# The first input of a two-layer kernel in eight stages of two column tiles, with keys and half of the values between the modulation units

## The chip, the cores and the metric

The kernel runs on one core of a Trainium2 chip. The metric is the time of the device for one execution, in microseconds (us). All matrix work is in fp32, done as three products of a reduced fp32 format, so one multiplication of a tile is three instructions on TensorE (PE). ScalarE (ACT) and VectorE (DVE) prepare operands and collect sums; the queue of SyncE (SP) issues nearly all loads from the chip's memory.

## The reference

Two layers run over a sequence of 256 rows (`x`) beside a context of 256 rows (`ctx`), both 2048 wide. Each layer first makes a shift, a scale and a gate out of a small condition vector, by a product with `w_ada` (2048 x 6144 per layer). Layer 0 is a gated linear attention with a short convolution; of the context it needs only the end states.

```python
m = jax.nn.silu(cond) @ w[:, :n * D_MODEL] + b[:n * D_MODEL]       # modulation
u  = x * (1.0 + sc) + sh            ;  uc = ctx_s * (1.0 + sc_c) + sh_c
k, v, rf, rb, q, ... = split_cols(u @ w_in_e[0], E_SIZES)          # keys 1024, values 1024, ranks 32, ...
s_f, s_b = context_states(uc @ w_in_e[0][:, :E_STATE_COLS], ...)   # keys, values, ranks of ctx
y  = even_mixer(u @ w_in_e[0], s_f, s_b, ...)   ; x = layer_norm(alpha * x + gt * y, ...)
y  = odd_mixer(u1 @ w_in_o[0], w_pool, ...)     ; x = layer_norm(alpha * x + gt * y, ...)
```

## The kernel before

The change lies in the first phase, which makes keys, ranks and a part of the values of layer 0, for `x` and `ctx` together. It walks over the 2048 input columns in tiles of 128 (16 tiles, `kt`). A **stage** is one or two of these tiles. `STAGES` gives their widths: one, one, and then seven times two.

For one stage, `stage_u` does the following. `mod_rows` (L274) multiplies the condition vectors with the stage's columns of `w_ada`, in **units** of 1 MB; a stage of two tiles has four units of eight tiles of 256 columns each, a stage of one tile has two units of sixteen tiles of 128 columns. `to_cols` copies the sum to `arow` (L285, ACT), turns it with PE (`adaT`, L288), and two DVE instructions add the bias (`modT`, L293 and L295). PE transposes the `x` and `ctx` columns (`px`, L389 and L390). ACT and DVE then make u (L392, L393), and split it into a high and a low part (`uxh`, `uch` on ACT L397 and L398; `uxl`, `ucl` on DVE L399 and L400). After every four tiles PE makes the four rank products (`pr`, L405), each in two passes.

`stage_k` makes the keys: for two halves of 512 columns and four blocks of rows, three instructions per tile (`kacc`, L190 to L192), so 24 per tile and 48 per stage of two. The weights come as raw loads and are split by ACT (`wh`, L152) and DVE (`wl`, L153). The sums are copied by ACT in the first stage (`knat`, L423), and added by DVE in the others (L425).

A **fill** (`v_fill`) multiplies two tiles with the first 512 columns of the values, 24 instructions (`vfill`), with its own split weights (`swh`, `swl`) and its sums in `vnat` (L454 copies on ACT, L456 adds on DVE). There are four fills, for the first eight tiles; the other eight tiles of these columns are done behind the first phase (`vacc`). Behind the first phase follow the turned keys (`nT`, L684), values, queries, gates, the recurrence, the output products and layer 1. The modulation of layer 1 and the gate of layer 0 are a background of 1 MB loads, each with four DVE sums (`aacc`, L533).

The raw loads of `w_ada` and of all weights (L138) go in one order through the queue of SP into a pool of four raw buffers of 1 MB; a load waits until its buffer's last reader is done. A scheduler lays the instructions of each engine into one order before the run, by priorities and by explicit "issue after" edges; on the chip each engine keeps that order.

## Time and profile before

| what | value |
|---|---|
| median of 3 runs | 1011.63 us (1009.72 to 1018.11) |
| the profiled execution | 1005.89 us, its span 1004.1 us |
| granted TensorE clock, mean of the span | 0.995 |
| TensorE busy | 958.9 us, 95% |
| VectorE busy | 807.0 us, 80% |
| ScalarE busy | 468.9 us, 47% |
| moved by DMA | 255.44 MB, mean 254 GB/s |

Times in the trace count from the start of the span. The times "start to start" of two matmuls matter more here than their durations, because matmuls overlap. A wait of an engine is the idle time ahead of an instruction, put down to what released it.

### The profile page before, as it was taken

To read this page: it belongs to the slowest core of one execution; us is meant where nothing else is said; L and a number is where in the kernel's file an instruction comes from. 1 tells how busy PE (TensorE), PEld (TensorE's weight loads), DVE (VectorE), ACT (ScalarE), POOL (GpSimd) and SP (SyncE) were. 2 spreads that over 40 slices of the span, in tenths; PEclk is the share of its full clock that TensorE was granted. 3 is DMA by queue.
4 is the path that set the end of the run, shared out by engine and by line. 5 is a ranking of instruction groups with operands and counts; after the bars stand their busy time and mean duration, and the time that the engine had idled before them with its cause. 6 is when DMAs were issued, how large, how long until landed. Compare 5 with 4: busy or idle time off the path is not lost.

```text
span 1004.1 us, 14346 instructions
## 1 busy us (share of the span) xinstructions
PE 958.9 (95%) x5654; PEld 757.0 (75%) x5654; DVE 807.0 (80%) x1172; ACT 468.9 (47%) x643; POOL 24.4 (2%) x56
## 2 busy tenths in 40 slices
PE   5899999999999999999999999999989999989995
PEld 4566756778878877877888788888778777768885
DVE  1555646989996999799999879997979997666676
ACT  2422214356675676246463344345745555435340
POOL 2000000000000000000000000000010001000000
PEclk9999999999999999999999999999999999999998
DMA  9987899567787586757766897985598998875532
GB/s 264 328 263 257 289 290 339 188 242 235 260 300 262 179 268 218 257 195 258 248 215 226 299 309 263 327 303 200 175 354 288 309 333 317 264 282 190 178 117 84
DMA packets 150371, 255.44 MB, mean 254 GB/s; under 512 B 5078, under 2 KB 46720, under 8 KB 150304
## 3 DMA queue, kind: packets, MB, share of 16 engines
q1 hardware_dynamic: 146592, 245.13, 72.5%
q0 software_dynamic: 2896, 8.72, 2.9%
q8 instruction: 44, 0.72, 0.3%
q10 hardware_dynamic: 816, 0.68, 0.3%
q14 instruction: 23, 0.19, 0.0%
HBM read 252.41 MB, written 2.10 MB: 253 GB/s over the span
## 4 chain that ended last, share of the span: by engine, by line
PE 49%; DVE 29%; DMA 15%; issue 4%; ACT 2%; SPq 0%; DVEq 0%; ACTq 0%
DMA raw<-in_w_ada_dram 12%; DVE wl L153 10%; DVE aacc L533 7%; PE oacc L190 5%; PE oacc L191 5%; PE oacc L192 5%; PE xacc L192 5%; PE xacc L191 5%; PE xacc L190 5%; PE ada L274 2%; DMA raw<-in_w_in_o_dram 2%; PE kacc L190 2%; PE kacc L192 2%; PE kacc L191 2%; PE pr L405 1%
## 5 line engine op out<-in xcount | busy, mean ns | idle before, releaser
L152 ACT CAST wh<-raw 128x1024 fp32r<-128x1024 f32 (+1 forms) x250 | 257.2, 1044 | 249.4 <-PE xacc L192 74.5
L153 DVE TENSOR_TENSOR wl<-raw,wh 128x1024 fp32r<-128x1024 f32 (+1 forms) x250 | 298.0, 1210 | 46.7 <-ACT wh L152 44.2
L533 DVE SCALAR_TENSOR_TENSOR aacc<-raw,sil,aacc 128x512 f32<-128x512 f32 x240 | 179.3, 747 | 30.8 <-DMA raw<-in_w_ada_dram 27.1
L190 PE MATMUL xacc<-wh,uxh 128*128 128x512 f32 x384 | 152.6, 397 | 0.0
L192 PE MATMUL xacc<-wh,uxl 128*128 128x512 f32 x384 | 151.5, 395 | 0.0
L191 PE MATMUL xacc<-wl,uxh 128*128 128x512 f32 x384 | 150.2, 391 | 0.5 <-DVE wl L153 0.4
L191 PEld LDWEIGHTS xacc<-wl,uxh 128*128 128x128 f32 x384 | 72.2, 188 | 16.3 <-DVE wl L153 1.3
L190 PEld LDWEIGHTS xacc<-wh,uxh 128*128 128x128 f32 x384 | 72.1, 188 | 15.5 <-ACT wh L152 0.5
L192 PEld LDWEIGHTS xacc<-wh,uxl 128*128 128x128 f32 x384 | 72.1, 188 | 15.3 <-issue 0.2
L425 DVE TENSOR_TENSOR knat<-kacc,knat 128x512 f32<-128x512 f32 x64 | 42.8, 685 | 34.7 <-PE kacc L192 34.5
L285 ACT COPY arow<-ada 128x256 f32<-128x256 f32 (+1 forms) x9 | 3.1, 349 | 100.6 <-PE ada L274 100.6
L274 PE MATMUL ada<-raw,sil 128*32 128x256 f32 (+1 forms) x576 | 36.2, 382 | 10.8 <-DMA raw<-in_w_ada_dram 10.8
L190 PE MATMUL xacc<-wh,u1h 128*128 128x512 f32 x112 | 44.9, 401 | 0.8 <-ACT u1h L1160 0.8
L190 PE MATMUL oacc<-wh,y1h 128*128 128x512 f32 (+1 forms) x120 | 45.5, 379 | 0.0
L191 PE MATMUL xacc<-wl,u1h 128*128 128x512 f32 x112 | 44.7, 399 | 0.5 <-DVE wl L153 0.4
L192 PE MATMUL oacc<-wh,y1l 128*128 128x512 f32 (+1 forms) x120 | 45.0, 375 | 0.0
L191 PE MATMUL oacc<-wl,y1h 128*128 128x512 f32 (+1 forms) x120 | 45.0, 375 | 0.0
L192 PE MATMUL xacc<-wh,u1l 128*128 128x512 f32 x112 | 44.5, 397 | 0.0
L274 PEld LDWEIGHTS ada<-raw,sil 128*32 128x32 f32 x576 | 17.4, 118 | 27.0 <-issue 12.0
L190 PE MATMUL kacc<-wh,uxh 128*128 128x512 f32 x64 | 26.8, 418 | 1.5 <-ACT uxh L397 1.5
L1221 PE MATMUL xacc<-wh,dm 128*128 128x512 f32 x64 | 25.7, 402 | 2.5 <-ACT wh L152 2.5
L190 PE MATMUL kacc<-wh,uch 128*128 128x512 f32 x64 | 26.4, 412 | 0.5 <-DVE knat L425 0.5
(339 smaller groups left out, 1866.6 us busy)
## 6 DMA issues: line engine op xcount, KB each, us to landing
raw<-in_w_ada_dram SPq DMA_DIRECT2D x96, 1024.0 KB, 6.3
raw<-in_w_in_e_dram SPq DMA_DIRECT2D x54, 1024.0 KB, 5.5
raw<-in_w_in_o_dram SPq DMA_DIRECT2D x32, 1024.0 KB, 7.2
raw<-in_w_out_e_dram SPq DMA_DIRECT2D x16, 1024.0 KB, 7.0
raw<-in_w_out_o_dram SPq DMA_DIRECT2D x16, 1024.0 KB, 5.1
raw<-in_w_in_e_dram SPq DMA_DIRECT2D x18, 512.0 KB, 7.0
raw<-in_w_pool_dram SPq DMA_DIRECT2D x4, 1024.0 KB, 7.7
gt<-in_b_ada_dram POOLq DMA_DIRECT2D x8, 256.0 KB, 4.1
```

The source lines that it names most:

```text
L152: nc.scalar.copy(h, r[:, j : j + w, :])
L153: nc.vector.tensor_tensor(out=l, in0=r[:, j : j + w, :], in1=h.bitcast(F32), op=ALU.subtract)
L190: nc.tensor.matmul(out=acc, lhsT=uh, rhs=wh, start=start, stop=False)
L191: nc.tensor.matmul(out=acc, lhsT=uh, rhs=wl, start=False, stop=False)
L192: nc.tensor.matmul(out=acc, lhsT=ul, rhs=wh, start=False, stop=stop)
L274: nc.tensor.matmul(out=ps[32 * g : 32 * g + 32, :], lhsT=sil[:, kt, 2 - 2 * half : 34 - 2 * half], rhs=r[:, j, :], start=half == 0 and kt ...
L285: arow_ins.append(nc.scalar.copy(a[:, :nw], ps))
L405: nc.tensor.matmul(out=pr[32 * g : 32 * g + 32, :], lhsT=wr[:, kk, :], rhs=quad_u[kk // 2][:, kk % 2, :], start=True, stop=True,)
L425: nc.vector.tensor_tensor(out=dst, in0=acc, in1=dst, op=ALU.add)
L533: e.scalar_tensor_tensor(out=a, in0=r[j], scalar=sc, in1=a, op0=ALU.mult, op1=ALU.add)
L1221: nc.tensor.matmul(out=accs[0], lhsT=dh, rhs=wh, start=f, stop=False)
```

## The change

The 16 tiles go in eight stages of two. There are eight fills, one for each stage, so the first 512 columns of the values are complete at the end of the first phase, and the two blocks of them behind it are gone. `stage_u` of the next stage is laid between the key and fill groups of the present one: `behind(unit)` puts each of its modulation units after a group that is given by `PLACE` (after 3/16, 6/16, 9/16 and 12/16 of the groups). The transposes come after the last unit but one of stage 0 and after the last unit in the others (with no explicit place for `adaT`), the rank products as one piece after the first group of the second key half. The loads of a stage's keys are issued ahead of its third unit's load (ahead of the fourth in stage 0). The splits of weights follow after the high parts of u. In the head, 25 products of a zero tile are put between the modulation units (`keep_warm`). One background unit (1 MB, four `aacc`) follows each of the stages 4 to 7.

```diff
-ADA_0 = {}
+ADA_0 = {i: 1 for i in range(4, 8)}
-FILLS = {2: [(0, 0, 2)], 4: [(0, 2, 2)], 6: [(0, 4, 2)], 8: [(0, 6, 2)]}
+FILLS = {k + 2: [(0, k, 2)] for k in range(0, KT, 2)}
+PLACE = 3
+STAGE_PRIO = 2000
-STAGES = (1, 1, 2, 2, 2, 2, 2, 2, 2)
+WARM = (7, 5, 3)
+STAGES = (2, 2, 2, 2, 2, 2, 2, 2)
...
+    def keep_warm(n, behind=None):
+        idle = mp([P, 256], "idle")
+        for _ in range(n):
+            with tc.issue_after(behind.ins) if behind else nullcontext():
+                nc.tensor.matmul(out=idle, lhsT=zero[:, 0:P], rhs=zero, start=True, stop=True)
...
-    def mod_rows(k0, n):
+    def mod_rows(k0, n, behind, between):
...
+                unit = half * (KT // nk) + kk // nk
+                if unit == 3 and k0 == 0:
+                    w_load(1)
+                elif unit == 2 and k0:
+                    w_load(min(len(specs), wst["u"] + 2))
                 r = load_unit(w_ada[0], kk, nk, c0, nw)
+                with behind(unit):
+                    for j in range(nk):
+                        kt = kk + j
+                        g = kt % 4
+                        ins = nc.tensor.matmul(
+                            out=ps[32 * g : 32 * g + 32, :], lhsT=sil[:, kt, 2 - 2 * half : 34 - 2 * half], rhs=r[:, j, :],
+                            start=half == 0 and kt < 4, stop=half == 1 and kt >= KT - 4,
+                        )
+                between(half, kk + nk, ins)
...
-    def stage_u(k0, n):
+    def stage_u(k0, n, groups):
...
+        pxs = {}
+
+        def transposes(j):
+            pxs[j] = mp([P, 512], "px")
+            for t in range(2):
+                nc.tensor.transpose(out=pxs[j][:, t * P : (t + 1) * P], in_=xs[:, t, j * P : (j + 1) * P], identity=ident)
+                nc.tensor.transpose(out=pxs[j][:, 256 + t * P : 256 + (t + 1) * P], in_=cs[:, t, j * P : (j + 1) * P], identity=ident)
+
+        def between(half, k, ins):
+            if (half, k) == (1, KT // 2 if k0 == 0 else KT):
+                with tc.issue_after(ins.ins):
+                    for j in range(n):
+                        transposes(j)
+            if k0 == 0:
+                keep_warm(WARM[2] if (half, k) == (1, KT) else WARM[1], ins)
+
+        def behind(unit):
+            if not groups:
+                return nullcontext()
+            return tc.issue_after(groups[(unit + 1) * len(groups) * PLACE // 16 - 1].ins)
+
...
         pt = to_cols(ps, w)
+        with tc.issue_after(arow_ins[-1].ins):
+            w_ahead(1, 1)
...
             if i == 3:
+                ranks_due.append(kt)
...
+        with tc.issue_after(behind.ins), prio(-2 * STAGE_PRIO):
+            first = product(3)
+            with tc.issue_after(first.ins):
+                for g in range(3):
+                    product(g)
...
+    def stage_k(k0, n, groups):
         for nb in range(2):
             parts = w_next((W_E, k0, n, nb * 512), 0, 0)
             for m in range(4):
                 acc = acc_bank("kacc")
                 for j in range(n):
-                    mm3(acc, utile(m, k0 + j), parts[j], j == 0, j == n - 1)
+                    ins = mm3(acc, utile(m, k0 + j), parts[j], j == 0, j == n - 1)
+                groups.append(ins)
+                if ranks_due and (nb, m) == (1, 0):
+                    ranks(ranks_due.pop(), ins)
...
+    starts = [sum(STAGES[:i]) for i in range(len(STAGES))]
+    groups = []
+    for i, (k0, n) in enumerate(zip(starts, STAGES)):
+        if i == 0:
+            stage_u(k0, n, [])
+            with tc.issue_after(h_ins[-1].ins):
+                w_ahead(3, 2)
+        if i + 1 < len(STAGES):
+            xcs[k0 + n] = load_xc(k0 + n, STAGES[i + 1])
+        groups = []
+        stage_k(k0, n, groups)
+        for f in FILLS.get(k0 + n, ()):
+            v_fill(*f, groups)
+        pump_ada(ADA_0.get(i, 0))
+        if i + 1 < len(STAGES):
+            with prio(-STAGE_PRIO):
+                stage_u(k0 + n, STAGES[i + 1], groups)
+                with tc.issue_after(h_ins[-1].ins):
+                    w_ahead(3, 2)
```

Three places show what this does to the order of the instructions; the names are tile and buffer numbers of the program.

In the queue of SP, at the start of the program, these loads stood before (the columns of `x` and `ctx` of the first stage go through another queue):

```order
L138 DMA raw_141<-in_w_ada_dram 128x16x128
L138 DMA raw_159<-in_w_ada_dram 128x16x128
L138 DMA raw_198<-in_w_in_e_dram 128x512
L138 DMA raw_204<-in_w_in_e_dram 128x512
L138 DMA raw_214<-in_w_ada_dram 128x16x128
L138 DMA raw_232<-in_w_ada_dram 128x16x128
L211 DMA xc_210<-in_x_dram 128x2x128
L212 DMA xc_210<-in_ctx_dram 128x2x128
```

and these stand there now:

```order
L141 DMA raw_151<-in_w_ada_dram 128x8x256
L141 DMA raw_167<-in_w_ada_dram 128x8x256
L141 DMA raw_183<-in_w_ada_dram 128x8x256
L141 DMA raw_209<-in_w_in_e_dram 128x2x512
L141 DMA raw_211<-in_w_ada_dram 128x8x256
L141 DMA raw_252<-in_w_in_e_dram 128x2x512
L141 DMA raw_258<-in_w_in_e_dram 128x2x512
L141 DMA raw_368<-in_w_ada_dram 128x8x256
L141 DMA raw_378<-in_w_ada_dram 128x8x256
```

All four units of stage 0 (`raw_151`, `raw_167`, `raw_183`, `raw_211`) come ahead of the first keys, where two units of half the columns came before; one key load of 0.5 MB (`raw_209`) lies among them. On DVE, the same place read before:

```order
L248 COPY colT<-pc_1_177 128x32
L293 SCALAR_TENSOR_TENSOR modT<-adaT_182,colT 128x2
L295 TENSOR_TENSOR modT<-adaT_182,colT 128x2
L153 TENSOR_TENSOR wl_201<-raw_198,wh_200 128x512
L153 TENSOR_TENSOR wl_207<-raw_204,wh_206 128x512
L393 TENSOR_SCALAR u_186<-px_187,modT 128x256
L399 TENSOR_TENSOR uxl_117<-u_186,uxh_116 128x256
L400 TENSOR_TENSOR ucl_119<-u_186,uch_118 128x256
```

and reads now:

```order
L156 TENSOR_TENSOR wl_234<-raw_209,wh_233 128x1024
L262 COPY colT<-pc_1_225 128x32
L314 SCALAR_TENSOR_TENSOR modT<-adaT_230,colT 128x2x2
L316 TENSOR_TENSOR modT<-adaT_230,colT 128x2x2
L435 TENSOR_SCALAR u_239<-px_193,modT 128x256
L435 TENSOR_SCALAR u_239<-px_198,modT 128x256
L441 TENSOR_TENSOR uxl_127<-u_239,uxh_126 128x256
L442 TENSOR_TENSOR ucl_129<-u_239,uch_128 128x256
```

The split `wl` of the first weights, 128x1024 in one, stands ahead of `colT` and `modT`, and there are two u instead of one ahead of the first low part. On ACT, in the order of the rows, the end of the first fill read before:

```order
L397 CAST uxh_116<-u_370 128x256
L152 CAST wh_489<-raw_487 128x1024
L398 CAST uch_118<-u_370 128x256
L454 COPY vnat_445<-vfill_449 128x512
L454 COPY vnat_446<-vfill_457 128x512
L454 COPY vnat_447<-vfill_465 128x512
L454 COPY vnat_448<-vfill_473 128x512
L285 COPY arow_542<-ada_496 128x256
L392 ACTIVATE u_549<-px_550,modT 128x256
L392 ACTIVATE u_549<-px_561,modT 128x256
L397 CAST uxh_120<-u_549 128x256
L398 CAST uch_122<-u_549 128x256
```

and reads now (`u_433` is the u of the stage 1, whose first keys come right behind `vfill_359` on PE):

```order
L511 COPY vnat_331<-vfill_335 128x512
L306 COPY arow_422<-ada_367 128x256
L155 CAST wh_427<-raw_388 128x1024
L511 COPY vnat_332<-vfill_343 128x512
L511 COPY vnat_333<-vfill_351 128x512
L511 COPY vnat_334<-vfill_359 128x512
L434 ACTIVATE u_433<-px_412,modT 128x256
L434 ACTIVATE u_433<-px_417,modT 128x256
L439 CAST uxh_126<-u_433 128x256
L440 CAST uch_128<-u_433 128x256
```

Three copies of the fill now stand between the split of the weights of stage 1 and its u. Before, the u of the keys that follow the fill (`u_370`) stood ahead of all four copies.

On DVE, at the stage whose modulation comes with the gate weights (`gate_weights`, `wp`), the rows before read:

```order
L293 SCALAR_TENSOR_TENSOR modT<-adaT_1286,colT 128x2x2
L295 TENSOR_TENSOR modT<-adaT_1286,colT 128x2x2
L425 TENSOR_TENSOR knat_134<-kacc_1330,knat_134 128x512
L425 TENSOR_TENSOR knat_135<-kacc_1338,knat_135 128x512
L153 TENSOR_TENSOR wl_1381<-raw_1378,wh_1380 128x1024
L425 TENSOR_TENSOR knat_132<-kacc_1346,knat_132 128x512
L425 TENSOR_TENSOR knat_133<-kacc_1354,knat_133 128x512
L425 TENSOR_TENSOR knat_134<-kacc_1362,knat_134 128x512
L153 TENSOR_TENSOR wl_1387<-raw_1384,wh_1386 128x1024
L425 TENSOR_TENSOR knat_135<-kacc_1370,knat_135 128x512
L437 TENSOR_TENSOR wp_1281<-wg_1276,wp_1281 32x1024
L393 TENSOR_SCALAR u_1291<-px_1292,modT 128x256
```

and now, with the fill of the stage before it (`vfill_1305` to `vfill_1329`) ahead:

```order
L513 TENSOR_TENSOR vnat_331<-vfill_1305,vnat_331 128x512
L488 MEMSET wg_1406 96x1024
L493 TENSOR_TENSOR wp_1403<-wg_1398,wp_1403 32x1024
L513 TENSOR_TENSOR vnat_332<-vfill_1313,vnat_332 128x512
L513 TENSOR_TENSOR vnat_333<-vfill_1321,vnat_333 128x512
L513 TENSOR_TENSOR vnat_334<-vfill_1329,vnat_334 128x512
L314 SCALAR_TENSOR_TENSOR modT<-adaT_1416,colT 128x2x2
L316 TENSOR_TENSOR modT<-adaT_1416,colT 128x2x2
L156 TENSOR_TENSOR wl_1420<-raw_1364,wh_1419 128x1024
L493 TENSOR_TENSOR wp_1411<-wg_1406,wp_1411 32x1024
L435 TENSOR_SCALAR u_1425<-px_1388,modT 128x256
```

Three adds of the fill stand ahead of `modT` now; the adds of keys that stood between `modT` and u are gone from there, and the split of the next keys' weights and the second `wp` stand in their place.

## Rows read from the trace of the kernel before

**Rows 1.** page, 1: busy time, share of the span and instructions of an engine

```profile
PE 958.9 (95%) x5654; PEld 757.0 (75%) x5654; DVE 807.0 (80%) x1172; ACT 468.9 (47%) x643; POOL 24.4 (2%) x56
```

**Rows 2.** page, 4: the chain of waits by engine

```profile
PE 49%; DVE 29%; DMA 15%; issue 4%; ACT 2%; SPq 0%; DVEq 0%; ACTq 0%
```

**Rows 3.** stretches: start:end, length, busy PE, PEld, DVE, ACT, POOL, PEclk, DMA, GB/s

```profile
16.95:194.24 177.29, 172.00 (x1117) 114.42 (x1118) 104.77 (x190) 49.95 (x91) 0.41 (x2) 1.00 0.88 284
64.00:86.00 22.00, 21.73 (x141) 14.52 (x141) 12.62 (x23) 5.46 (x10) 0.00 (x0) 1.00 0.87 286
```

**Rows 4.** waits of PE, ahead of 194.24 and behind: total us, times, longest

```profile
PE ada L274 <- DMA raw<-in_w_ada_dram: 10.8, 6, 4.6
...
PE yT L968 <- DVE y L962: 4.1, 3, 2.0
PE y1T L1279 <- DVE gate L1326: 3.3, 1, 3.3
```

**Rows 5.** the head in order of time: start us, us, instruction, idle before

```profile
11.99 1.30 PE L274 MATMUL ada<-raw,sil 128*32 128x128 f32 x20 [2.46 <-DMA raw<-in_w_ada_dram]
...
14.00 0.27 ACT L285 COPY arow<-ada 128x128 f32<-128x128 f32 x1 [9.54 <-PE ada L274]
...
14.16 1.14 ACT L152 CAST wh<-raw 128x512 fp32r<-128x512 f32 x2
15.09 1.28 DVE L153 TENSOR_TENSOR wl<-raw,wh 128x512 fp32r<-128x512 f32 x2
15.90 0.56 ACT L392 ACTIVATE u<-px,modT 128x256 f32<-128x256 f32 x1 [0.60 <-PE px L390]
16.49 0.40 ACT L397 CAST uxh<-u 128x256 fp32r<-128x256 f32 x1
16.95 0.80 PE L190 MATMUL kacc<-wh,uxh 128*128 128x512 f32 x1 [1.09 <-ACT uxh L397]
```

**Rows 6.** bytes moved from 0 to 45 us, in 40 slices of 1.125 us

```profile
GB/s 0 15 191 308 323 287 288 290 282 305 362 315 300 180 156 289 291 291 289 307 361 361 350 348 346 348 346 348 349 350 349 350 367 356 352 401 279 256 376 308
```

**Rows 7.** PE in two stages: start us, us, instruction

```profile
63.58 0.51 PE L288 MATMUL adaT<-sel,arow 128*128 128x4 f32 x4
64.77 0.48 PE L192 MATMUL kacc<-wh,uxl 128*128 128x512 f32 x1
65.78 0.39 PE L190 MATMUL kacc<-wh,uch 128*128 128x512 f32 x1
...
68.28 0.39 PE L192 MATMUL kacc<-wh,ucl 128*128 128x512 f32 x1
...
76.86 1.07 PE L274 MATMUL ada<-raw,sil 128*32 128x256 f32 x16
77.86 0.50 PE L192 MATMUL kacc<-wh,uxl 128*128 128x512 f32 x1
...
133.70 1.05 PE L405 MATMUL pr<-u,wr_acc 128*32 128x512 f32 x4
134.69 0.50 PE L190 MATMUL kacc<-wh,uch 128*128 128x512 f32 x1
```

**Rows 8.** the end of the first phase, PE

```profile
194.24 1.47 PE L684 MATMUL nT<-ident,knat 128*128 128x128 f32 x12
```

**Rows 9.** groups of the first phase: count, busy us, mean ns, idle before

```profile
L454 ACT COPY vnat<-vfill 128x512 f32<-128x512 f32 x4 | 2.3, 584 | 2.4 <-PE vfill L192 2.4
L456 DVE TENSOR_TENSOR vnat<-vfill,vnat 128x512 f32<-128x512 f32 x12 | 8.3, 689 | 2.5 <-PE vfill L192 2.4
L153 DVE TENSOR_TENSOR swl<-raw,swh 128x1024 fp32r<-128x1024 f32 x4 | 4.9, 1218 | 0.4 <-ACT swh L152 0.4
```

**Rows 10.** PE behind its longest wait of the later phases

```profile
884.35 1.09 PE L1279 MATMUL y1T<-ident,gate 128*128 128x128 f32 x8 [3.31 <-DVE gate L1326]
...
885.93 0.63 PE L192 MATMUL xacc<-wh,u1l 128*128 128x512 f32 x1
...
888.49 0.60 PE L192 MATMUL xacc<-wh,u1l 128*128 128x512 f32 x1
```

More of the change, by code (lines that the diff above doesn't have):

```diff
@@ L1 @@
 import math
-from contextlib import ExitStack, contextmanager
+from contextlib import ExitStack, contextmanager, nullcontext
 import concourse.bass as bass
@@ L191, in mm3 @@
         nc.tensor.matmul(out=acc, lhsT=uh, rhs=wl, start=False, stop=False)
-        nc.tensor.matmul(out=acc, lhsT=ul, rhs=wh, start=False, stop=stop)
+        return nc.tensor.matmul(out=acc, lhsT=ul, rhs=wh, start=False, stop=stop)
     rows0 = slot([32, P], F32, "rows0")
@@ L269, in mod_rows @@
             for kk in range(0, KT, nk):
-                r = load_unit(w_ada[0], kk, nk, c0, nw)
-                for j in range(nk):
-                    kt = kk + j
-                    g = kt % 4
-                    nc.tensor.matmul(
-                        out=ps[32 * g : 32 * g + 32, :], lhsT=sil[:, kt, 2 - 2 * half : 34 - 2 * half], rhs=r[:, j, :],
-                        start=half == 0 and kt < 4, stop=half == 1 and kt >= KT - 4,
-                    )
+                unit = half * (KT // nk) + kk // nk
[3 more added lines that the diff above has]
+                    w_load(min(len(specs), wst["u"] + 2))
+                r = load_unit(w_ada[0], kk, nk, c0, nw)
+                with behind(unit):
[7 more added lines that the diff above has]
+                between(half, kk + nk, ins)
         return ps
-    arow_ins = []
+    arow_ins, h_ins = [], []
     def to_cols(ps, nw):
@@ L370, in stage_u @@
         xs, cs = xc[:, 0:2, :], xc[:, 2:4, :]
-        ps = mod_rows(k0, n)
+        pxs = {}
[15 more added lines that the diff above has]
+            return tc.issue_after(groups[(unit + 1) * len(groups) * PLACE // 16 - 1].ins)
+        ps = mod_rows(k0, n, behind, between)
         if k0 == 0:
@@ L386, in stage_u @@
             u = quad_u[-1]
-            px = mp([P, 512], "px")
-            for t in range(2):
-                nc.tensor.transpose(out=px[:, t * P : (t + 1) * P], in_=xs[:, t, j * P : (j + 1) * P], identity=ident)
-                nc.tensor.transpose(out=px[:, 256 + t * P : 256 + (t + 1) * P], in_=cs[:, t, j * P : (j + 1) * P], identity=ident)
+            px = pxs[j]
             ux, uc = u[:, kt % 2, 0:256], u[:, kt % 2, 256:512]
@@ L401, in stage_u, with ranks, product @@
             if i == 3:
-                pr = mp([P, 512], "pr")
-                for g in range(4):
-                    kk = kt - 3 + g
-                    nc.tensor.matmul(
-                        out=pr[32 * g : 32 * g + 32, :], lhsT=wr[:, kk, :], rhs=quad_u[kk // 2][:, kk % 2, :],
-                        start=True, stop=True,
-                    )
-                if q == 0:
-                    nc.vector.tensor_copy(r_acc, pr)
-                else:
-                    nc.vector.tensor_tensor(out=r_acc, in0=pr, in1=r_acc, op=ALU.add)
-    def stage_k(k0, n):
+                ranks_due.append(kt)
+    ranks_due = []
+    def ranks(kt, behind):
+        pr = mp([P, 512], "pr")
+        def product(g):
+            kk = kt - 3 + g
+            return nc.tensor.matmul(
+                out=pr[32 * g : 32 * g + 32, :], lhsT=wr[:, kk, :], rhs=quad_u[kk // 2][:, kk % 2, :], start=True, stop=True)
+        with tc.issue_after(behind.ins), prio(-2 * STAGE_PRIO):
[3 more added lines that the diff above has]
+                    product(g)
+        if kt == 3:
+            nc.vector.tensor_copy(r_acc, pr)
+        else:
+            nc.vector.tensor_tensor(out=r_acc, in0=pr, in1=r_acc, op=ALU.add)
+    def stage_k(k0, n, groups):
         for nb in range(2):
@@ L440, with v_fill @@
     vnat = []
-    def v_fill(nb, kt, nk):
+    def v_fill(nb, kt, nk, groups):
         parts = w_next((W_E, kt, nk, 1024 + nb * 512), 0, 0)
@@ L450, in v_fill @@
                 for j in range(nk):
-                    mm3(acc, utile(m, kt + j), parts[j], j == 0, j == nk - 1)
+                    ins = mm3(acc, utile(m, kt + j), parts[j], j == 0, j == nk - 1)
+                groups.append(ins)
                 dst = vnat[m][:, nb * 512 : (nb + 1) * 512]
@@ L771 @@
     for nb in range(2):
+        if not V_Q[nb]:
+            continue
         accs = [acc_bank("vacc") for _ in range(4)]
```

21 lines of the change are left out of this document (4 added, 17 removed).

## Prediction

> **What bounds the kernel.** I read the page first: TensorE is busy for 95% of the span [rows 1], and it is the largest share of the chain of waits, with DVE at 29% and DMA at 15% [rows 2]. Next I looked at the first phase by stretches, since the edit is there: from the first key product at 16.95 to the first turned key at 194.24 [rows 8] PE is busy for 172.0 of 177.3 us, at full granted clock [rows 3]. The waits of PE say where the rest is: modulation units that wait for their load, 10.8 us in six waits [rows 4]. 4.6 us of that is the longest, ahead of the first unit, and 2.5 us the next, ahead of the second [rows 4, 5]; so only some 3.7 us of load waits lie inside the phase. The timeline gives prices: twelve instructions of keys start between 65.78 and 68.28, one each 0.227 us [rows 7]. That is the price of a matmul here, not its duration of 0.39.
>
> So PE is packed, and a change of order can win only the head, the slow clock at its end, and the small waits. Let me count what these are. Behind 16.95 the phase holds 384 key products (87.2 us), 96 of fills (21.8), 30 units of modulation at 1.1 (33.0), seven blocks and two half blocks of transposes (about 10.4), and four rank groups at 3.3 (13.2): 165.6 us. 177.3 - 165.6 = 11.7 us is lost, and 16.95 us ahead of it.
>
> **Prices, step by step.**
>
> *Point of comparison.* The change moves 96 value products from behind the phase into it, at 0.227 each 21.8 us. Later they are missing, so they cost nothing in sum, as long as PE is packed in both places. The equal of 194.24 is then 216.0.
>
> *Head.* Four units of 1.05 MB now come ahead of the first key product, with 0.52 MB of keys, 0.52 MB of `x` and `ctx` and, by their shapes, 0.37 MB of rank weights and small rows: 5.6 MB. The slices of bytes moved add up to 3.34 MB at 13.5 us [rows 6]. The other 2.26 MB take 6.5 us at the 349 GB/s of the later slices, 7.5 at 300: 20.0 to 21.0. If the whole head went at 349 from 3.4 us on, it would be 18.8. I take 20.2, and 1.0 for the unit on PE [rows 7]: 21.2. From there, the chain. In the trace of before it took 2.95 us from `arow` to the first key product [rows 5]. Now DVE's split of 1.22 us (the `swl` of the same size) [rows 9] stands ahead of `modT` and itself waits for ACT's split of about 1.05 (two halves took 1.14) [rows 5]. Summed: `arow` 0.4, 1.05, 1.22, column copy and `modT` 0.5, u 0.56 and the second one 0.5, `uxh` 0.46 until the product starts: 4.7. First key product at 25.9, with bounds of 24.5 and 27.5.
>
> *Work behind it.* Keys 87.2; fills, now 192 products, 43.6; 28 units at 1.00 from start to next start and 0.1 at the switch into them, 30.8 [rows 7]; seven blocks of `adaT` and transposes at 1.19 and 0.1, 9.1 [rows 7]. The rank products came in three pieces of 1.0 to 1.1 per group (the first piece 0.99) [rows 7]; as one piece I put 2.5, between 2.0 and 3.3: 10.0. Sum 180.7.
>
> *New waits.* Each engine keeps its order. At the end of the first fill ACT has three copies of the fill ahead of u of stage 1, whose keys follow at once: last copy 0.58 [rows 9], u 0.56 and 0.5, `uxh` 0.4 [rows 5], hand-overs: 2.2 us. At the gate weights, DVE's add of the last fill block, 0.69 [rows 9], is ahead of `modT`, and then the same chain: 2.8 us. Before, keys that needed none of this covered both. Three smaller ones are read alike: 1.3 between stages 4 and 5, where the background's sums stand ahead; 1.3 ahead of the last fill, for its split of 1.22 [rows 9]; 1.7 for loads in stage 6, about one wait of the kind that was 10.8 / 6 = 1.8 [rows 4]. The other borders I put at 0.7 together. Sum 10.0. The bounds are 4 (only the two chains, half covered by products already queued) and 18 (each of the six other borders as long as the shorter chain, less overlap).
>
> *The 25 zero products.* They fill waits for loads of the head, where PE had 4.6 and 2.5 us of idle time [rows 4, 5]: nothing. If they delayed each unit by one of them, it would be under 1 us, inside the bounds of the head. What they are to bring is the clock. Behind a wait of 3.31 us PE's products started 0.427 us apart (885.93 to 888.49, six starts) instead of 0.227 [rows 10, 7], for eight instructions in a row: 1.6 us. The wait at the end of the head is of that kind (4.7 us with about 1.5 us of transposes, zero products and `adaT` inside); I put half of 1.6, so 0.8, with ends of 0 and 1.6. [...]
>
> *Moved DVE and ACT work.* 16 more adds of the fills, eight fewer of the keys and four fewer of the values, at 0.69: +2.8 us of DVE, and four background units are summed earlier; DVE is busy for 12.6 of 22.0 us in such a stage [rows 3], so this is covered, and so are ACT's 5.5 of 22.0.
>
> *Later phases.* They lose 96 products and what stands with them. Waits for DVE there are short (4.1 and 3.3 us in the two largest groups) [rows 4]. I take 0, with ends of -4 and +3.
>
> *Sum.* 25.9 + 180.7 + 10.0 = 216.6, against 216.0: +0.6; with the clock +1.4. The profiled execution took 1005.9 us, so 1007.3; the median of the runs shown stands 5.7 us above that execution, so as a median **1013.0 us**. The differences that this kernel's measurement can tell from none are about 1%, 10 us; by that, this is no change.
>
> **Rivals.**
>
> *Faster.* The waits don't appear and loads come early: 18.8 + 1.0 + 4.7 = 24.5, ranks at 2.0 (178.7), waits 4.0, full clock: 207.2, or -8.8, and with the -4 of the later phases -12.8. As a median 999 to 1003. For it speaks that the chain's six other waits in the trace were small; against it that the first product is 8 us later than before, whatever happens behind it. I give it 0.24, half of it beyond 10 us.
>
> *Slower: loads bound the stages with a background unit.* In stages 4 to 7 one stage loads four units, 1.05 of keys, 0.52 of values, 0.52 of `x` and `ctx` and one background unit: 7.3 MB. At 349 GB/s [rows 6] that is 21.0 us, of about 22.6 us of PE work; a stage before moved 286 GB/s in 22.0 us [rows 3], 6.3 MB. There are only four raw buffers, and the background's is freed by DVE's sums, in DVE's order. From the point where a load of a stage's last units is held by more than the 1.6 us to spare, each stage waits. Priced at 1.8 us [rows 4] for two units in each of four stages it is 14.4 us: 1013.0 + 14.4 = 1027. I give it 0.2, of which 0.15 beyond 10 us.
>
> *Nothing moves.* The two chains are covered, the head costs more, and the one pays for the other: 1005 to 1010, chance 0.1. My own sum, from 1006 to 1022 with its bounds, has 0.46; 0.02 of it I put beyond 10 us.
>
> **Numbers.** Faster by over 1%: half of 0.24 and a little of later phases, 0.13. Slower: 0.15 and 0.02, 0.17. Within 1%: 0.70. The range goes from 1001 (a part of the faster case) to 1027 (the price of the slower one); some 0.2 is left outside.
>
> **What would show it.** First key product at 24.5 to 27.5, and the first few products 0.43 apart or not. First `nT` at about 216.6 plus the clock (207 in the faster case, 231 in the slower). Among the waits of PE, `kacc` for `uxh` or u once at the border of stages 0 and 1 and once at the gate weights, 2 to 3 us each; if these are absent, my reading of the order is wrong. Waits of `ada` for loads in stages 4 to 7 above 5 us in sum would speak for the slower case. If behind `nT` the rest of the program takes more or less than the 809.9 - 21.8 = 788.1 us that are left of 1004.1 - 194.24, by over 4 us, the later phases were not neutral, and the prediction fails there.

## The result and the profile after

The change ran 20 times at a median of **1017.44 us** (1011.29 to 1021.69), beside the kernel before at 1011.61 us (20 runs, 1006.58 to 1018.11): ratio **1.0065** [1.005, 1.008]. That is slower by some 6 us, within the 1% that was forecast as no change; the predicted 1013.0 us is 4.4 us short. The profiled execution took 1019.4 us, its span 1017.6 us, with a mean granted clock of 0.98 where the profile of before had 0.995.

The page of the change first: busy times, the granted clock in forty slices, and the shares of the chain of waits.

```profile
PE 969.7 (95%) x5640; PEld 771.7 (76%) x5640; DVE 807.6 (79%) x1173; ACT 469.3 (46%) x640; POOL 24.4 (2%) x56
...
PEclk9999999899999999999999999999999899999998
...
PE 51%; DVE 25%; DMA 15%; issue 4%; ACT 4%; DVEq 0%; ACTq 0%
```

Beside [rows 1, 2] this looks the same: PE still binds. PE was busy for 10.8 us longer, with 14 instructions fewer, but that alone says little, because the work is not the same: the 25 zero products of the head, which the kernel before does not have, are 13.9 us of it (count, busy us, mean ns), and the rank products went down from 12.2 to 4.3 us.

```profile
L239 PE MATMUL idle<-zero 128*128 128x256 f32 x50 | 13.9, 433 | 0.0
```

What the clock costs is read from stretches, below. The waits of PE come first (total us, times, longest).

```profile
PE ada L294 <- DMA raw<-in_w_ada_dram: 7.7, 9, 2.4
PE kacc L193 <- ACT uxh L439: 6.2, 3, 2.3
...
PE y1T L1341 <- DVE gate L1379: 3.7, 1, 3.7
PE y1T L1341 <- DVE gate L1388: 2.9, 1, 2.9
...
PE xacc L1283 <- ACT dm L1239: 1.8, 1, 1.8
PE xacc L1284 <- DVE dm L1240: 1.3, 1, 1.3
...
PE vfill L194 <- DVE swl L156: 0.9, 1, 0.9
```

Against [rows 4], loads cost 3 us less in all. That is the head: behind it the waits for loads are 5.5 us, where they were 3.7. The 6.2 us of waits for `uxh`, one at each of three places, stand where the kernel before had 1.5:

```profile
PE kacc L190 <- ACT uxh L397: 1.5, 2, 1.1
```

These places stand below in the order of time (start us, us, instruction, idle time before): the head, the border of stages 0 and 1, the gate weights with a load just before, and the end of the phase.

```profile
21.34 1.07 PE L294 MATMUL ada<-raw,sil 128*32 128x256 f32 x16 [0.16 <-DMA raw<-in_w_ada_dram]
...
26.89 0.50 PE L193 MATMUL kacc<-wh,uxh 128*128 128x512 f32 x1 [2.28 <-ACT uxh L439]
...
28.04 0.63 PE L194 MATMUL kacc<-wl,uxh 128*128 128x512 f32 x1
28.47 0.63 PE L195 MATMUL kacc<-wh,uxl 128*128 128x512 f32 x1
...
54.01 0.50 PE L193 MATMUL kacc<-wh,uxh 128*128 128x512 f32 x1 [1.89 <-ACT uxh L439]
54.99 0.63 PE L194 MATMUL kacc<-wl,uxh 128*128 128x512 f32 x1
...
170.03 1.42 PE L294 MATMUL ada<-raw,sil 128*32 128x256 f32 x16 [2.43 <-DMA raw<-in_w_ada_dram]
...
180.45 0.50 PE L193 MATMUL kacc<-wh,uxh 128*128 128x512 f32 x1 [1.99 <-ACT uxh L439]
182.78 0.80 PE L195 MATMUL kacc<-wh,uxl 128*128 128x512 f32 x1 [1.01 <-DVE uxl L441]
...
219.57 0.60 PE L744 MATMUL nT<-ident,knat 128*128 128x128 f32 x4
```

Behind the first two of these waits for `uxh` products last 0.63 us instead of 0.39, and start 0.43 us apart (28.04 to 28.47) instead of 0.227 [rows 7]. The stretches around the four longest waits of the phase show less than full clock, and behind each of these waits it is 0.50 for a time, called half clock below (28 to 30, 55 to 57, 172 to 174 and 184 to 186 us). The stretches (start:end, length, busy time of PE, PEld, DVE, ACT and POOL with counts, PEclk, DMA share, GB/s):

```profile
24.00:32.00 8.00, 5.72 (x29) 4.23 (x32) 4.94 (x11) 4.24 (x9) 0.00 (x0) 0.79 1.05 334
52.00:60.00 8.00, 6.11 (x20) 4.79 (x20) 4.95 (x9) 4.61 (x9) 0.00 (x0) 0.79 0.74 229
164.00:176.00 12.00, 9.57 (x58) 6.18 (x57) 6.24 (x8) 1.05 (x1) 0.00 (x0) 0.86 0.82 243
176.00:188.00 12.00, 9.00 (x48) 6.00 (x44) 8.87 (x16) 6.58 (x11) 0.00 (x0) 0.72 0.79 246
```

Before, the granted clock of the whole first phase reads 1.00 [rows 3], though its first key products start 0.43 us apart as well (17.54, 17.97, 18.40).

**A count for the comparisons.** From each trace I took the starts of the products of keys, values, output and the like (some 3,530; units of modulation, transposes, ranks and zero products are not counted), and set the start of the n-th against that in the profile of before, wherever the fills stand. At product 600 the kernel before has also done 2.3 us of other work (`pz`, `adaS`, `rsel`) that comes later in the change; by product 1000 this is level but for 0.8 us. The second table is worked out from slices of 4 us: (1 - granted clock) x 4, summed up to 990 us. It is an upper bound for what the clock cost, since PE is idle in a part of these slices.

| n | place | before, us | before again (e9) | change | e10 | e5 | e11 |
|---|---|---|---|---|---|---|---|
| 600 | behind the first phase | 228.6 | +2.9 | +6.2 | +0.1 | +1.1 | +1.1 |
| 1000 | behind the values | 330.0 | +3.3 | +6.3 | +0.4 | +1.5 | +1.1 |
| 2300 | ahead of layer 1 | 695.0 | +6.1 | +7.5 | +3.6 | +5.4 | +1.0 |
| 2400 | behind its first products | 722.5 | +6.1 | +12.6 | +6.5 | +11.6 | +2.5 |
| 2600 | ahead of `y1T` | 774.0 | +8.2 | +9.2 | +5.8 | +8.2 | +2.4 |
| 2700 | behind it | 799.7 | +7.9 | +14.5 | +7.7 | +13.7 | +3.5 |
| 3530 | the end | 992.0 | +6.6 | +13.4 | +7.3 | +12.6 | +0.4 |

| | before | before again | change | e10 | e5 | e11 |
|---|---|---|---|---|---|---|
| lost at half clock, at most, us | 1.7 | 8.5 | 17.0 | 10.0 | 10.2 | 0.0 |

The profile of the change thus shows 13.4 us, over twice what the medians differ by: its execution lies 2.0 us above its median, that of before 5.7 us below its own. Three steps make it: the first phase, the start of layer 1 (products 2300 to 2400: 27.5 us before, 32.6 now) and `y1T` (2600 to 2700: 25.7 and 31.1).

In layer 1 the place is DVE's order. Ahead of layer 1's first `dm` products before, DVE does this (start us, us, instruction):

```profile
708.72 0.68 DVE L1178 TENSOR_TENSOR dm<-d,dm 128x512 fp32r<-128x512 f32 x1
709.40 1.23 DVE L153 TENSOR_TENSOR wl<-raw,wh 128x1024 fp32r<-128x1024 f32 x1
```

and in the change:

```profile
717.98 1.23 DVE L156 TENSOR_TENSOR wl<-raw,wh 128x1024 fp32r<-128x1024 f32 x1
...
719.72 2.35 DVE L156 TENSOR_TENSOR wl<-raw,wh 128x1024 fp32r<-128x1024 f32 x2
721.99 1.02 DVE L1240 TENSOR_TENSOR dm<-d,dm 128x512 fp32r<-128x512 f32 x2
```

The `dm` step stands behind three more splits of weights now, though the change touches nothing in layer 1; PE waits 1.8 and 1.3 us for it (rows of waits above) and runs at half clock behind that (0.50 from 724 to 727 us).

### The profile page after: what moved, and what is told of

Read it like the earlier page. It is cut to its first block, busy times and chain, and to the rows that moved or that the text cites. A ratio compares the mean times of both kernels' runs of the same rounds, so it can differ in the third digit from the quotient of the medians.

```text
span 1017.6 us, 14314 instructions
## 1 busy us (share of the span) xinstructions
PE 969.7 (95%) x5640; PEld 771.7 (76%) x5640; DVE 807.6 (79%) x1173; ACT 469.3 (46%) x640; POOL 24.4 (2%) x56
## 4 chain that ended last, share of the span: by engine, by line
PE 51%; DVE 25%; DMA 15%; issue 4%; ACT 4%; DVEq 0%; ACTq 0%
DMA raw<-in_w_ada_dram 12%; DVE wl L156 10%; PE oacc L193 6%; PE oacc L195 6%; PE oacc L194 6%; DVE aacc L590 5%; PE xacc L195 4%; PE xacc L193 3%; PE xacc L194 3%; PE ada L294 2%; PE kacc L195 2%; PE kacc L193 2%; PE kacc L194 2%; DMA raw<-in_w_in_e_dram 2%; DMA raw<-in_w_in_o_dram 2%
## 5 line engine op out<-in xcount | busy, mean ns | idle before, releaser
L155 ACT CAST wh<-raw 128x1024 fp32r<-128x1024 f32 x244 | 253.3, 1052 | 222.9 <-PE xacc L195 72.9
L156 DVE TENSOR_TENSOR wl<-raw,wh 128x1024 fp32r<-128x1024 f32 x244 | 293.6, 1219 | 73.9 <-ACT wh L155 71.3
L306 ACT COPY arow<-ada 128x256 f32<-128x256 f32 x8 | 3.0, 372 | 117.8 <-PE ada L294 117.8
L481 DVE TENSOR_TENSOR knat<-kacc,knat 128x512 f32<-128x512 f32 x56 | 37.8, 687 | 24.4 <-PE kacc L195 24.2
L294 PE MATMUL ada<-raw,sil 128*32 128x256 f32 x512 | 34.5, 390 | 7.9 <-DMA raw<-in_w_ada_dram 7.7
L513 DVE TENSOR_TENSOR vnat<-vfill,vnat 128x512 f32<-128x512 f32 x28 | 19.1, 686 | 19.0 <-PE vfill L195 19.0
L294 PEld LDWEIGHTS ada<-raw,sil 128*32 128x32 f32 x512 | 14.4, 110 | 26.0 <-DMA raw<-in_w_ada_dram 11.9
L156 DVE TENSOR_TENSOR swl<-raw,swh 128x1024 fp32r<-128x1024 f32 x20 | 23.8, 1216 | 7.9 <-ACT swh L155 7.9
```

The source lines that it names most:

```text
L155: nc.scalar.copy(h, r[:, j : j + w, :])
L156: nc.vector.tensor_tensor(out=l, in0=r[:, j : j + w, :], in1=h.bitcast(F32), op=ALU.subtract)
L294: ins = nc.tensor.matmul(out=ps[32 * g : 32 * g + 32, :], lhsT=sil[:, kt, 2 - 2 * half : 34 - 2 * half], rhs=r[:, j, :], start=half == 0 a ...
L306: arow_ins.append(nc.scalar.copy(a[:, :nw], ps))
L481: nc.vector.tensor_tensor(out=dst, in0=acc, in1=dst, op=ALU.add)
L513: nc.vector.tensor_tensor(out=dst, in0=acc, in1=dst, op=ALU.add)
```

## The experiments

Each kernel ran beside the kernel before, on the same chip; the change did not run beside them, so it is compared by its ratio. "Zero products" are products of a zero tile with 256 columns into an accumulator that is cleared afterwards, 0.48 us each at a granted clock of 1.00 (e2 has five of them in 2.42 us; the trace shows each as two matmuls).

### One suspect each: e1 to e4

**e1, copies of the first fill on DVE.**

```diff
-                    nc.scalar.copy(dst, acc)
+                    nc.vector.tensor_copy(dst, acc)
```

> The change with one edit: the first fill's four copies are made by DVE, not by ACT, so they no longer stand ahead of u of stage 1 on ACT. Theory A (the 6.5 us that the change loses are waits in the engines' order at a few borders of stages, each followed by some 1.6 us of half clock on TensorE): the wait of kacc for uxh at 54 us (1.9) goes, a wait of about 1 us for the low part of u may come in its place, the clock stays up there: 2 to 3.5 us less than the change, 1.003 to 1.0045 times before. Theory B (the eight fills cost by themselves, wherever their copies are made): as the change, 1.0065. Theory C (loads, with the background units of stages 4 to 7): as the change, 1.0065.

Measured 1015.51 us, 1.0053 [1.0031, 1.0075]. The wait at the border moved as the order says: the first key product starts at once, and a later one waits for DVE.

```profile
51.52 0.39 PE L193 MATMUL kacc<-wh,uxh 128*128 128x512 f32 x1
...
53.71 0.50 PE L195 MATMUL kacc<-wh,uxl 128*128 128x512 f32 x1 [1.12 <-DVE uxl L441]
```

The clock from 52 to 60 us was 1.00. So the three copies in ACT's queue were what held `uxh`. In the total this is not told from the change.

**e2, five zero products in the head's chain of waits.**

```diff
+        if k0 == 0:
+            keep_warm(5, adaT_ins[-1])
```

> The change with five more zero products behind adaT of stage 0, to fill the 2.3 us in which PE waits for the first u. Theory A: first keys at about 26.9 as in the change, but 0.23 us apart from the start instead of 0.43 for nine products: 1.6 us less than the change, 1.005 times before. If the zero products push the first keys back or the clock falls all the same (rival): no less than the change, 1.0065 or more. Theories B and C: no part of the loss is here, at most 0.5 us less.

Measured 1016.41 us, 1.0068 [1.0041, 1.0096].

```profile
24.93 2.42 PE L239 MATMUL idle<-zero 128*128 128x256 f32 x10 [0.59 <-DVE colT L262]
27.00 0.58 PE L193 MATMUL kacc<-wh,uxh 128*128 128x512 f32 x1
27.64 0.39 PE L195 MATMUL kacc<-wh,uxl 128*128 128x512 f32 x1
```

The first key product comes 0.1 us later (27.00 against 26.89) and the keys go at full pitch from the second on (27.42, 27.64, 27.87; the clock is 1.00 from 24 to 32 us); between products 9 and 40 this profile is 1.4 us ahead of the change. Then a unit, which in the change starts at 41.88 without a wait, waits for its load:

```profile
42.08 1.07 PE L294 MATMUL ada<-raw,sil 128*32 128x256 f32 x16 [1.51 <-DMA raw<-in_w_ada_dram]
```

By product 50 the lead is gone. The total again can't tell it.

**e3, gate weights behind the high parts of u.**

```diff
         if k0 == GW_AT:
-            gate_weights()
...
+            with tc.issue_after(h_ins[-1].ins):
+                gate_weights()
```

> The change with the gate weights (loads, casts and subtractions of wp) behind the high parts of u of their stage instead of ahead of its bias. Theory A: the waits of kacc at 180 to 183 us (2.0 for uxh, 1.0 for uxl) fall below 1 us in sum, and so does the half clock behind them: 3 to 4.5 us less than the change, 1.002 to 1.0035 times before. Theories B and C: nothing changes beyond 1 us, 1.0055 to 1.0065.

Measured 1021.46 us, 1.0101 [1.0072, 1.013]: a miss. At product 450 the kernel was 8.3 us ahead of before, where the change was 2.3 behind. Then a load came late:

```profile
195.01 1.93 PE L294 MATMUL ada<-raw,sil 128*32 128x256 f32 x16 [5.63 <-DMA raw<-in_w_ada_dram]
```

At product 600 it stood at +6.7, as the change does. As in e2, what PE was ahead was given back at a load. The edit also moves the loads of the gate weights, and no run shows whether that made this one late.

**e4, no background units in the first phase.**

```diff
-ADA_0 = {i: 1 for i in range(4, 8)}
+ADA_0 = {}
```

> The change without the background units in stages 4 to 7 (they come later, as before the change). Theory C: the 2.4 us wait of a modulation unit for its load at 170 us goes, with the half clock behind it, and the small load waits of stages 4 to 7 too: 4 us or more less than the change, 1.0025 times before or less, unless the later phases give it back. Theory A: that one wait goes with its half clock, 3 to 4 us, but the 16 DVE sums come back behind the first phase, where DVE is busy nearly throughout: 0 to 4 us less, 1.0025 to 1.0065. Theory B: as the change.

Measured 1026.47 us, 1.0176 [1.0141, 1.0211]. The first phase was 5 us shorter than the change's (+1.1 at product 600), but +20.7 stood at product 2400: at 700 us the order has new waits, the longest of which is

```profile
PE xacc L1283 <- ACT dm L1239: 4.9, 1, 4.9
```

The background's loads press on the first phase only a little: without them the waits for loads are 6.4 us there instead of 7.7. Most of the 5 us goes with the clock, which cost at most 5.1 us there instead of 8.4 (worked out as in the second table). The units have to go somewhere, though, and a cut in the first phase has changed the order 500 us later.

### Waits filled, and fills halved: e5 to e8

**e5, zero products at the three borders.** `zero_products` issues them right behind a given product: five in the head, four ahead of the keys of stage 1, six at the gate weights.

```diff
+BORDERS = {0: 5, 2: 4, 12: 6}
...
+                if (nb, m) == (0, 0) and k0 in BORDERS:
+                    if k0 != 2:
+                        last_mm[0] = adaT_ins[-1]
+                    zero_products(acc[:, 0:256], BORDERS[k0])
```

> The change with zero products of 0.49 us each in the three waits of the first phase for u: five behind adaT of stage 0, four behind the last product of the first fill, six behind adaT of the stage with the gate weights. They change no wait of DVE, ACT or DMA; PE is only busy where it waited. Theory D (new; the waits themselves are small, the loss is the half clock that follows every wait of PE of 2 us or more): no granted clock below 0.9 at 24 to 32, 52 to 60 and 180 to 188 us, 1.6 us less for each of the first two and up to 3 for the third: about 6 us less than the change, 1.0005 times before. Theory A' (the waits themselves cost, the clock little): at most 1 us less, 1.0055 to 1.0065, or more, if the products reach beyond the waits.

Measured 1017.81 us, 1.0081 [1.0056, 1.0107]. Its stretches, as those of the change above:

```profile
24.00:32.00 8.00, 7.98 (x47) 5.77 (x47) 4.62 (x11) 4.36 (x9) 0.00 (x0) 1.00 1.03 325
52.00:60.00 8.00, 7.83 (x38) 5.94 (x40) 7.19 (x12) 3.67 (x8) 0.00 (x0) 1.00 0.62 193
164.00:176.00 12.00, 9.32 (x70) 6.64 (x69) 5.98 (x10) 3.69 (x7) 0.00 (x0) 1.00 0.81 240
176.00:188.00 12.00, 10.85 (x64) 7.61 (x66) 10.78 (x18) 2.90 (x5) 0.00 (x0) 1.00 0.91 283
```

All four falls are gone and product 600 starts 5.1 us earlier than in the change: products were added to the phase, and it got shorter. e11, with the same zero products, repeats it (+1.1, no fall). But only three of the four waits were filled. The wait for a load stood as before, even a little longer (2.43 in the change), and this time no fall followed:

```profile
166.84 1.07 PE L303 MATMUL ada<-raw,sil 128*32 128x256 f32 x16 [2.52 <-DMA raw<-in_w_ada_dram]
```

So the two runs show that the first phase in the change's profile lost most of these 6 us to the clock, and that the clock stayed at 1.00 around the waits that were filled; they don't show that every execution of the change loses them (e10 below). And the total isn't lower; the profile is back at +11.6 by product 2400. Of the 4.3 us that are lost between 600 and 2300 a fall of the clock from 436 to 444 us has 1.7 at most; the 6.2 us up to 2400 are the `dm` step.

**e6, the same with 20 more at four later waits.**

```diff
+            if (hp, t) == (0, 0):                      # yT
+                zero_products(pt[:, 0:2, :], 5)
...
+        if n0 == 0:                                    # xacc, dm
+            zero_products(accs[0][:, 0:256], 4)
...
+            if c2 == 0 and g in (0, 2):                # y1T
+                zero_products(pt[:, 0, :], 6 if g == 0 else 5)
```

> As the one before, and also zero products where the later phases wait in the trace of the change: five ahead of the first yT (440 us), four ahead of the first products of layer 1's d block (720), six and five ahead of y1T (792 and 896). Theory D: the dips of the clock at these four places go too, 1.5 us each, so about 12 us less than the change: 0.9945 times before. Theory A': as the change, or slower by up to the 9.7 us that the 20 products last, where no wait covers them: 1.0065 to 1.016.

Measured 1024.84 us, 1.015 [1.0116, 1.0183]: a miss, by a wait that no other kernel had so far:

```profile
PE xacc L201 <- ACT swh L156: 7.1, 1, 7.1
```

**e7, the 20 later ones of e6 in the kernel before**, which has no `BORDERS`.

```diff
+            if (hp, t) == (0, 0):
+                zero_products(pt[:, 0:2, :], 5)
...
+        if n0 == 0:
+            zero_products(accs[0][:, 0:256], 4)
...
+            if c2 == 0 and g in (0, 2):
+                zero_products(pt[:, 0, :], 6 if g == 0 else 5)
```

> The kernel before with the same 20 zero products in its later phases and nothing else. Theory D: the dip at 884 us goes (1.6 us), and those that runs near the median have beyond the profiled one: 1.5 to 4 us less, 0.996 to 0.9985 times before. If the later phases of before hold no waits of 2 us besides 884: the products cost up to 6 us where nothing waits, 0.9985 to 1.005. Theory A': 1.000 to 1.006.

Measured 1019.1 us, 1.0097 [1.0074, 1.0121], with the same wait:

```profile
PE xacc L197 <- ACT swh L152: 7.0, 1, 7.0
```

So it is made by the 20 products and not by the first phase. They change the scheduler's order on ACT and DVE.

**e8, fills for the first eight tiles only, as before.**

```diff
-FILLS = {k + 2: [(0, k, 2)] for k in range(0, KT, 2)}
+FILLS = {k + 2: [(0, k, 2)] for k in range(0, 8, 2)}
```

> The change with four fills (stages 0 to 3) as before, and the other two blocks of the values behind the first phase. Theory B (the moved values cost): most of the loss goes, 1.000 to 1.002. Theory D: the borders 0 to 1 and the load wait at 170 stay or move, the border at the gate weights loses the fill's adds ahead of modT, so that its 3 us of waits and its half clock may go: 0 to 4 us less, 1.0025 to 1.0065.

Measured 1023.22 us, 1.0147 [1.0116, 1.0179]. Without the second four fills the first phase got worse (+15.4 at product 600):

```profile
PE ada L294 <- DMA raw<-in_w_ada_dram: 13.0, 11, 3.6
PE kacc L193 <- ACT uxh L439: 10.5, 5, 2.9
```

In this order the fills are cover, not cost: they stand between the keys of one stage and those of the next.

### Chance and order: e9 to e12

**e9, the kernel before, profiled again.** No edit.

> The kernel before once more, for a second profile: the first one's execution took 1005.9 us, 5.7 less than the median of all. Theory E (half clock behind waits makes the difference between runs too): an execution near the median shows more stretches below 0.97 than the one at 884 us, among the waits of the trace that are about 2 us long (yT near 440, the first products of layer 1 near 720, y1T near 785). If the missing 5 us are spread evenly (rival): no such stretch, and the gap to the first profile grows steadily along the span.

1012.46 us, clock 0.988. The same program shows falls that its first profile has not: it is 2.9 us later at product 600 and 6.1 at 2300. The first comes at a wait for a load that both executions have, here of 2.54 us, there of 2.02:

```profile
39.87 1.07 PE L274 MATMUL ada<-raw,sil 128*32 128x256 f32 x16 [2.54 <-DMA raw<-in_w_ada_dram]
```

From 36 to 48 us the clock was 0.72 in this execution, and 1.00 in the first. The gap to the first profile grows at its falls and not evenly. The waits ahead of them are 0.5 to 0.8 us longer too, so how much of the 6.6 us is the clock (at most 8.5 - 1.7 = 6.8) isn't told.

**e10, `dm` ahead of the splits.**

```diff
-    row_steps()
+    with prio(-1500):
+        row_steps()
```

> The change with one edit behind the first phase: the differences of neighbouring rows for layer 1 (d on DVE, dm on ACT and DVE) get a higher priority, so DVE makes the first low part of dm ahead of four splits of weights, as in the kernel before; the rest up to that place is the change's order word for word. Theory F (half of what the change loses in its profile is a new order at the hand-over to layer 1 and at y1T, which nobody wrote): the waits of 1.8 and 1.3 us at 721 us go, with their 1.5 us of half clock, and y1T comes eight products later, which takes its wait from 3.7 to about 2: 5 to 8 us less than the change, 0.9985 to 1.0015 times before. If the later phases take the time back, as they seem to have done with the fill of the first phase: 1.005 or more.

Measured 1015.15 us, 1.0056 [1.0033, 1.008]. The step moved up and PE waits for it no more:

```profile
711.27 1.02 DVE L1240 TENSOR_TENSOR dm<-d,dm 128x512 fp32r<-128x512 f32 x2
```

Products 2300 to 2400 take 30.3 us instead of 32.6, and 2600 to 2700 27.7 instead of 31.1. In the total about 1 us less than the change can't be told from none; the forecast gain was too large. The first phase of this profile teaches something else. Its order is that of the change word for word, and at the border of stages 0 and 1 it waits the same 1.89 us for `uxh`:

```profile
53.45 0.50 PE L193 MATMUL kacc<-wh,uxh 128*128 128x512 f32 x1 [1.89 <-ACT uxh L439]
54.26 0.40 PE L194 MATMUL kacc<-wl,uxh 128*128 128x512 f32 x1
```

There the change fell to half clock; here the next product lasts 0.40 us. This profile is at +0.1 by product 600, that of the change at +6.2. Its clock fell twice in the phase (0.79 from 24 to 32 us, 0.86 from 176 to 188), that of the change four times, and 2.1 us of the difference are shorter waits for loads (5.6 us instead of 7.7). Up to 713 us the two programs have one order on every engine, so this is what executions of the change differ by.

**e11, e5 and e10 together.**

```diff
+BORDERS = {0: 5, 2: 4, 12: 6}
...
-    row_steps()
+    with prio(-1500):
+        row_steps()
```

> Both: the zero products in the three waits of the first phase and the priority for dm. Theories D and F together: the first phase ends about 5 us earlier than in the change, and nothing gives it back at 720 and 795: 9 to 13 us less than the change, 0.994 to 0.9975 times before. If the end is set by another engine from layer 1 on (rival): as the run with the priority alone.

Measured 1012.18 us, **1.0023** [0.9999, 1.0048]: level with before, and some 4 us below the change; less than forecast. In its profile (1006.39 us) no slice ahead of the end is below full clock:

```profile
PEclk9999999999999999999999999999999999999998
```

**e12, e11 with e1 and zero products at `yT` and `y1T`.** Against e11:

```diff
-BORDERS = {0: 5, 2: 4, 12: 6}
+BORDERS = {0: 5, 2: 2, 12: 6}
...
-                    nc.scalar.copy(dst, acc)
+                    nc.vector.tensor_copy(dst, acc)
...
+            if (hp, t) == (0, 0):
+                zero_products(pt[:, 0:2, :], 4)
...
+            if c2 == 0 and g == 2:
+                zero_products(pt[:, 0, :], 4)
```

> The last run's two edits (zero products in the waits of the first phase, priority for dm), the first fill's copies on DVE (so only two zero products at that border), and four zero products each ahead of the first yT and of the y1T that waits near 896 us. Theory D: against the run with both edits about 1 us less at the first border, 1 at yT and 2 to 3 at y1T: 0.997 to 1.000 times before, so at least equal to it. If a new order of the later phases brings new waits, as in the two runs with 20 zero products: 1.003 or more.

Measured 1017.7 us, 1.0067 [1.0038, 1.0096]: a miss. Its head waits 2.0 us for a load and the clock falls (0.81 from 20 to 24 us, 0.76 from 24 to 28), and it falls again at 712, 753 and 804 us (0.58, 0.62 and 0.57 in the slices from 712, 752 and 804). The waits at these three places are not new. e11 has them as long and without a fall; of the last one, e11 first and then e12:

```profile
796.15 0.88 PE L1355 MATMUL y1T<-ident,gate 128*128 128x128 f32 x6 [1.91 <-DVE gate L1393]
...
803.11 0.88 PE L1359 MATMUL y1T<-ident,gate 128*128 128x128 f32 x6 [1.89 <-DVE gate L1397]
```

So the two profiles differ in part by chance; why the median is 5 us above that of e11 stays open. No version beat the kernel before.

## Why the prediction was right, and by how much it missed

**The frame held.** PE binds, the moved fills cost nothing by themselves (e8: without them it gets worse), and of the change as a whole little is seen in the total. The forecast sum was +1.4 us, the runs gave about +6: right in kind, 4.4 us short.

**Head.** First key product at 26.89, forecast 25.9, bounds 24.5 to 27.5. The last unit of the head started at 21.34; I had its end at 21.2. The chain behind it held.

**Work behind the head: right by luck.** I had the rank products as one piece at 2.5 us, and at 2.0 at least. They took 0.88:

```profile
62.64 1.08 PE L454 MATMUL pr<-u,wr_acc 128*32 128x512 f32 x8
63.52 1.27 PE L294 MATMUL ada<-raw,sil 128*32 128x256 f32 x20
```

That is 3.6 us in four groups instead of 10.0. Keys, fills and units, on the other hand, took 167.2 us in e11, where the clock never fell in this phase (from start to next start, idle time left out), against 87.2 + 43.6 + 30.8 = 161.6: the first product behind a switch or a wait takes some 0.34 us and not 0.227 (31.03 to 31.37 behind a unit in e2, 53.45 to 53.78 behind a wait in e10). The two errors cancel: 180.1 found, 180.7 forecast.

**New waits.** Forecast and found: 2.2 and 1.89 us at the border of stages 0 and 1; 2.8 and 1.99 + 1.01 at the gate weights; 1.7 and 2.43 for a load in stage 6; 1.3 and 0.9 for the split of the last fill. The 1.3 between stages 4 and 5 didn't show. From the first key product to the last fill the idle time is 11.3 us, forecast 10.0, but 5.5 of it are waits for loads, for which I had 1.7. Reading each engine's order gave place and size; e1 showed the cause of the first.

**Clock: the mis-sized term.** I charged half a fall, 0.8 us, for the head alone, and priced the other waits as idle time only. In its profile the change fell at four waits of 1.9 to 2.4 us. Three of the falls have about the price that I had worked out from [rows 10] (eight products at 0.427 instead of 0.227, 1.6 us); by the stretches above they cost at most 1.7 each, and the one at the gate weights, which lasted twice as long, 3.4; that makes 8.4. Measured as the work above, the phase took 187.6 us in the change and 180.1 in e11, so the four cost 7.5. Filling three of them, with the fourth gone by chance, brought 5.1 net in e5. The other executions say how often: e10, with the same order, fell only at 28 and at 176 to 184. Against the profile of before, the first phase thus costs between 0 and 6 us by the execution.

First `nT` came at 219.57, forecast 216.6 plus the clock, but 22 fills stand behind it. With them, and without the `nT` among them, the phase ended at 225.8, which is 8.4 us behind 216.6 + 0.8: the head 1.0, the waits 1.3, the clock 6.7, the work -0.6.

**Later phases: the other mis-sized term.** I took 0, with ends of -4 and +3. By the sign that I had set, they were not neutral: behind the first `nT` stand 1017.6 - 219.57 = 798.1 us instead of 788.1, and only 5.0 of the difference are the 22 fills. In the two profiles the rest behind product 600 is 13.4 - 6.2 = 7.2 us longer, 5.1 at layer 1's start and 5.4 at `y1T`, less what is given back between. I had argued from the work that moves, and the work wasn't the point: the scheduler lays a list in which everything downstream shifts. e10 shows the first of these two places by undoing it. Part of the 7 us is chance, since before itself has such falls (e9: +2.4 at 440 us, +2.1 at 750, with a clock of 0.79 from 436 to 444 and from 748 to 756).

**The slower rival** (loads bound the stages with a background unit) fell by its own sign: behind 120 us, where stages 4 to 7 lie, the waits of `ada` are 3.8 us, below the 5 that I had set.

```profile
PE ada L294 <- DMA raw<-in_w_ada_dram: 3.8, 3, 2.4
```

Without the background units (e4) waits for loads were 1.3 us less in the phase, not the 14.4 of the rival. The faster rival fell too: the waits came.

**The medians, by the clock.** The mean granted clock of the 20 runs of the change was 0.9812, of before 0.9912 (23 runs beside e1 to e4). Among those 23 runs of the unchanged kernel 0.001 of clock goes with 0.8 us. By that, an estimate, 0.010 would be 8 us, more than the 6 that were measured: at the same clock the change would be level or some 2 us ahead. e11, with the clock at 0.9902 (0.9905 in the runs beside it), is level. But this is a correlation, and it doesn't carry every run: e12, at 0.9882 against 0.9906, would be 2 us behind by it, and was 7.

**Open.** How the 6 us of the medians divide between the first phase and layer 1: e5 and e10 alone moved the total too little to tell, and only together gave 4 us. Nor is it settled why zero products that make the first phase 5 us shorter leave little of it at product 2300 (+5.4 in e5, but +1.0 in e11).

## What to carry to other kernels

Price a wait of a packed TensorE twice: its idle time, and a fall of the clock behind it, here 1.6 us, once twice that, and so as much as the wait itself; then ask in how many executions it falls. A fall that is gone in one profile of an edited kernel isn't yet cured by the edit. An edit of a scheduled kernel is also an edit of every order behind it: before costing the later phases at nothing, compare the orders there, at the places where an engine is waited for. And a single profile of before may be its lucky one: the range of its runs (1006.58 to 1018.11) was as wide as the effects that were argued about.

## What the runs showed of the hardware

I had not expected that one wait of one length is sometimes followed by half clock and sometimes not: 1.89 us at 54 us in the change (fell) and at 53.5 us in e10 (did not); 2.02 and 2.54 us at 39 us in two executions of before (only the longer one fell). The waits of 2.9 us and more at `y1T` of the change were followed by a low clock (0.50 from 796 to 800 us, 0.71 from 896 to 900), as was the one of 3.31 us before (0.50 from 886 to 888) [rows 10]. But e11 waited as long at `yT` and kept its clock (the change first, which fell to 0.50 from 444 to 447 us, then e11, with 1.00 from 436 to 448):

```profile
444.03 0.66 PE L1030 MATMUL yT<-ident,y 128*128 128x128 f32 x2 [3.16 <-DVE y L1024]
...
439.48 0.41 PE L1043 MATMUL yT<-ident,y 128*128 128x128 f32 x2 [3.30 <-DVE y L1037]
```

So the rule of Theory D, half clock behind every wait of 2 us or more, does not hold. What decides whether a fall follows, no run here shows. Where zero products filled all three waits of the first phase for `uxh`, the clock read 1.00 through the phase in e5, e6 and e11; in e12 it fell once, behind the wait for a load in the head. At the three borders I count, over all profiles of the change's kind, 16 waits of 1.9 to 2.3 us that were left open, with a fall behind 13 of them, and 13 that were filled (e2, e5, e6, e11, e12), with a fall behind none.
